# A hybrid encoder layer on one core: memory of its own for the output product's splits, FNet sums over even and odd columns, Conformer taps emitted one per quarter block

## The chip, the cores and the metric

The kernel runs on one core of a Trainium2 chip. Its time is the device time of one execution in microseconds (us); of several executions the median counts. One more execution is recorded by the hardware profiler: the profile and its trace. In it, PE is TensorE's matmuls and PEld its weight loads, DVE is VectorE, ACT is ScalarE, POOL is GpSimd, SP is the queue that issues most transfers, and L112 is line 112 of the kernel.

## What is computed

One layer over 512 positions of width 2048, in float32. A normalised `h` goes through one input projection of 11264 columns into four groups of 1024 channels and a gate; the groups are normalised, gated, and projected back:

```python
proj = h @ w_in
a, f, hy, q, gate = split(proj)                  # 2G, G, 3G, G, 4G columns, G = 1024
u = a_val * sigmoid(a_gate)                      # Conformer
u = depthwise_conv(u, conv_dw_w, conv_dw_b)      # 31 taps
y_a = silu(layer_norm(u)) @ conv_pw_w + conv_pw_b
ff = fft2(f, norm="ortho").real                  # FNet
y_b = ff @ fnet_w + fnet_b
hy = depthwise_conv(hy, hy_short_w, hy_short_b)  # Hyena, 3 taps
v, x1, x2 = split(hy)
for o, g_o in enumerate((x1, x2)):
    z = g_o * long_conv(z, kf[:, o], hy_skip[o]) # z is v at first
y_c = z
y_m = attention(q, mem_n @ mem_wk, mem_n @ mem_wv)
y = rms_norm(concat(y_a, y_b, y_c, y_m), per group) * silu(gate)
out = x + rms_norm(y @ w_out, post_g)
```

## The kernel before, in words

Channels stand on the 128 partitions and positions on the 512 columns, so a group is eight channel tiles (`CT`). To keep float32 accuracy, each operand of a large product is split in two parts: `split` (L79, L80) writes the high part with a ScalarE copy and the low part with a VectorE subtraction, and `mm3` (L112 to L114) makes three matmuls of them, high by high, high by low and low by high. `load` (L87) brings a weight block into one of three staging buffers, and `wload` splits it; `wload_dma` (L106 to L108) does so with a transfer that adds on the way, for the Hyena projections. `project(b)` (L313) makes one projection of 128 output channels: 48 matmuls of 512 columns in four quarters of 12, and after each quarter it advances a generator `fill` if it is given one.

There is no hand-written order: the program is written stage by stage, a scheduler sets each engine's queue from it, and a tile of a memory pool that reuses a buffer waits for the last reader of the old contents. A pool that is opened when another is closed takes over its memory, and waits likewise. The stages around the change:

- Hyena loop (`for ct in range(CT)`): three projections with a short convolution (`short`, L548, L549), then two `long_conv`. A `long_conv` goes: sum and difference `pq` on VectorE (L568, L569), four transposes on TensorE (L573), split `tH`, `tL`, 24 matmuls of 256 columns, products with the filter on VectorE, split `wwH`, `wwL`, matmuls again, four transposes (L624), and the output with its gate (L629, L630). Then `group_square` squares the result on ScalarE (L484) and adds it on POOL (L485) to `gaccC`. In four of the eight tiles (`CONV1`) a Conformer projection (`conv_proj`) and its 31 taps (`conv_taps`, L525, 30 operations of VectorE) follow. After the loop the projections left in `early` are made (`project_early`).
- FNet: 16 blocks of `w_f` are folded and multiplied (L681 to L697); in block 1 `group_norm` takes column sums of `gaccC` (L158) and spreads the scale with four small matmuls on `diag` (L152, L153). Then the transform over the positions: cosine tables `cg` (four chunks of 128 and a chunk of alternating signs) by the folded `eeH`, `eeL`, 30 matmuls of two columns (L743, L744), and sine tables `sg` by `ooH`, `ooL`. `out_product` multiplies with the FNet weights (L798 to L801).
- Conformer layer norm (pool `wp5`): the mean is subtracted (L952) in eight tiles, and `group_square` sums the squares in `vacc`; column sums of it (L158) come after the gate projection that follows. `lnt` holds mean, scale and two squares. The pointwise product sums its squares in `gaccA` likewise. Last, `group_scale` (L500) and a product with the early gates (L998) finish the group in 15 operations.
- Output product (pool `wp4`, opened when `wp5` is closed): in five rounds, 32 channel tiles `y` are split into `jh`, `jl` (three buffers each) and multiplied with `wo`.

Of the kernel before, what the change touches and what calls it, by code (L numbers as in the profile page):

```python
# [12 lines left out]
F32R = mybir.dt.float32r  # L13
# [7 lines left out]
P = 128  # L21
# [4 lines left out]
KD = D // P  # L26
# [12 lines left out]
C3 = 2.0 * math.pi - C1 - float(np.float32(C2))  # L39


@with_exitstack
def encoder_kernel(ctx: ExitStack, tc: tile.TileContext, a: dict, out: bass.AP):
# [26 lines left out]
    def pg():  # L70
        return psg.tile([P, 512], F32, tag="pg", name=nm("pg"))
# [289 lines left out]
    def query_early(i):  # L361
        ps = project(40 + i)
# [4 lines left out]
    def gate_early(i):  # L367
        ps = project(48 + i)
# [191 lines left out]
    def long_conv(z, g, dst, o, ct):  # L560
# [8 lines left out]
        dve.tensor_tensor(pq[:, 1], z0, z1, op=sub)  # L569
        pt = pg()  # L570
# [5 lines left out]
        split(tH, tL, pt)  # L576

# [31 lines left out]
        split(wH, wL, w_)  # L609
        pd = pg()  # L610
# [9 lines left out]
        dve.tensor_tensor(th_[:, 1], pdv[:, 0], dif, op=sub)  # L620
        pc = pg()
# [10 lines left out]
    gacc = cst.tile([P, 512], F32, tag="gacc", name="gaccC", bufs=2)  # L632
    for ct in range(CT):
        v = short(16 + 3 * ct, ct)
        x1 = short(16 + 3 * ct + 1, CT + ct)
        x2 = short(16 + 3 * ct + 2, 2 * CT + ct)
        z = kb[1][:, 2 + ct % 2, :]
        long_conv(v, x1, z, 0, ct)
        y = yC[ct // 4][:, ct % 4, :]
        long_conv(z, x2, y, 1, ct)  # L640
        group_square(y, gacc, wt("pp", bufs=3), ct == 0)
        if ct in CONV1:
            conv_proj(CONV1.index(ct), ub)
            conv_taps(CONV1.index(ct), ub)
    project_early(len(early))
# [81 lines left out]
    NS = ((0, 128), (128, 256), (130, 258))  # L727
    psT = [pg() for _ in range(3)]
    psX = pg()
    for c in range(5):  # L730
        raw = load(a["cg"][c], 512)
        th, tl = wsplit(raw[:, 0:512])
        for n in range(3):
            s = slice(*NS[n])
            if c < 4:
                mm3(psT[n], eeH[:, c, s], eeL[:, c, s], th, tl, c == 0, False)
            else:
                pe.matmul(psT[n], eeH[:, c, s], th, start=False, stop=False)
                pe.matmul(psT[n], eeL[:, c, s], th, start=False, stop=True)
# [51 lines left out]
    def out_product():  # L791
        for hf in range(2):
            psE = [pg() for _ in range(4)]
            psO = [pg() for _ in range(2)]
            for k in range(4):
# [177 lines left out]
    for hf in range(2):  # L973
# [54 lines left out]
    for r, ms in rounds:  # L1028
# [5 lines left out]
        for kp in range(16):  # L1034
# [12 lines left out]
            for kk in range(2):  # L1047
# [11 lines left out]
                jh = wt("jh", dt=F32R, bufs=3)  # L1059
                jl = wt("jl", dt=F32R, bufs=3)  # L1060
# [16 lines left out]
def _tables():  # L1077
# [10 lines left out]
    c = np.arange(512)  # L1088
    ang = 2.0 * np.pi * (np.outer(c, c) % 1024) / 1024.0
    alt = np.tile((-1.0) ** c / P, (P, 1))  # L1090
    t["cg"] = np.concatenate([np.cos(ang).reshape(4, P, 512), alt[None]])
    t["sg"] = np.sin(ang).reshape(4, P, 512)
# [24 lines left out]
def _arrange(inp):  # L1117
# [24 lines left out]
    r["w_f"] = np.concatenate([wf[:, :512], wf[:, mir]], axis=1).reshape(KD, P, 1024)  # L1142
# [7 lines left out]
    r["fw"] = np.stack([fw[:512], fw[mir]]).reshape(2, 4, P, 2, 512).transpose(3, 1, 2, 0, 4).reshape(2, 4, P, 1024)  # L1150
# [46 lines left out]
```

## Time and profile before

| | us |
|---|---|
| three runs | 1713.63, 1719.39, 1721.88 |
| median | 1719.39 |
| the profiled execution, its own time | 1716.29 |
| its span in the trace | 1714.5 |
| TensorE busy, of the span | 1655.3 (97%) |
| VectorE busy | 1221.9 (71%) |
| ScalarE busy | 813.6 (47%) |
| GpSimd busy | 189.9 (11%) |

A busy TensorE need not be at its peak: matmuls are pipelined, so one row's duration is longer than the distance to the next, and what a matmul costs is read from the distance of two starts. The granted clock is given in parts of 2.4 GHz; 0.50 is the lower level, 1.2 GHz. "[11.19 <-ACT jh L79]" behind a row says how long the engine had been idle before it and which instruction ended that.

### The profile page before, as it was taken

Reading aid. Unit: us, or ns where it says so; the run is one execution under the profiler, and the core shown is the slowest. Engines: PE = TensorE matmul, PEld = TensorE weight load, DVE = VectorE, ACT = ScalarE, POOL = GpSimd, SP = SyncE. Lnnn points to the kernel's source line nnn. Section 1 sums busy time; section 2 is a strip of 40 time slices with the busy share of each in tenths; the row PEclk is TensorE's granted clock in tenths of the full one; section 3 lists DMA queues with packets and bytes.
Section 4 is the critical chain, followed back from the end, with each engine's and each line's share of the span. In section 5 each row is a group of like instructions: output and inputs, shape, how many; then the busy total and the mean of one; then the engine's idle time right before and its main releaser. Section 6 shows DMA issues by size and latency. Waiting matters only on the chain.

```text
span 1714.5 us, 21887 instructions
## 1 busy us (share of the span) xinstructions
PE 1655.3 (97%) x8201; PEld 1386.6 (81%) x8201; DVE 1221.9 (71%) x1835; ACT 813.6 (47%) x1185; POOL 189.9 (11%) x146
## 2 busy tenths in 40 slices
PE   7999999999999999999999999999999699999997
PEld 5997888887777778878888888888878588888876
DVE  7866987378797887989874979985562545454586
ACT  6645655344343443424344355445454434444564
POOL 5101422011020120100000020100212000000000
PEclk9999999999999999999999999999999899999999
DMA  8654545768576684623434334232123523222355
GB/s 290 227 185 156 160 139 158 218 155 176 136 171 150 146 181 126 137 93 106 134 105 133 105 124 153 81 111 86 62 98 109 193 98 102 93 101 98 128 203 179
DMA packets 87487, 240.27 MB, mean 140 GB/s; under 512 B 8915, under 2 KB 26579, under 8 KB 86869
## 3 DMA queue, kind: packets, MB, share of 16 engines
q1 hardware_dynamic: 80468, 213.70, 38.6%
q0 software_dynamic: 6912, 25.17, 7.9%
q8 instruction: 64, 1.05, 0.2%
q14 instruction: 43, 0.34, 0.1%
HBM read 220.21 MB, written 18.63 MB: 139 GB/s over the span
## 4 chain that ended last, share of the span: by engine, by line
PE 78%; DVE 14%; DMA 2%; issue 2%; ACT 2%; POOL 1%; SPq 0%; DVEq 0%; ACTq 0%; POOLq 0%
PE pf L114 14%; PE pf L112 14%; PE pf L113 14%; PE pg L113 11%; PE pg L112 11%; PE pg L114 11%; DVE y L525 5%; DVE wl L80 2%; DVE yc L629 1%; DMA raw<-in_wv_dram 1%; POOL vacc L485 1%; ACT wh L79 1%; DMA wl<-in_w_std_dram 1%; DVE y L630 1%; DVE pq L568 1%
## 5 line engine op out<-in xcount | busy, mean ns | idle before, releaser
L112 PE MATMUL pf<-hH,wh 128*128 128x512 f32 x1280 | 505.6, 395 | 0.0
L114 PE MATMUL pf<-hH,wl 128*128 128x512 f32 x1280 | 502.7, 393 | 0.3 <-DMA wl<-in_w_std_dram 0.3
L113 PE MATMUL pf<-hL,wh 128*128 128x512 f32 x1280 | 502.1, 392 | 0.0
L80 DVE TENSOR_TENSOR wl<-raw,wh 128x1024 fp32r<-128x1024 f32 (+1 forms) x240 | 304.0, 1269 | 151.6 <-ACT wh L79 151.0
L79 ACT ACTIVATE wh<-raw 128x1024 fp32r<-128x1024 f32 (+1 forms) x240 | 247.5, 1033 | 231.3 <-PE pf L113 140.8
L114 PEld LDWEIGHTS pf<-hH,wl 128*128 128x128 f32 x1280 | 241.5, 189 | 49.6 <-DMA wl<-in_w_std_dram 0.7
L113 PEld LDWEIGHTS pf<-hL,wh 128*128 128x128 f32 x1280 | 241.9, 189 | 46.9 <-issue 0.2
L112 PEld LDWEIGHTS pf<-hH,wh 128*128 128x128 f32 x1280 | 241.7, 189 | 46.9 <-issue 0.5
L80 DVE TENSOR_TENSOR jl<-y,jh 128x512 fp32r<-128x512 f32 (+1 forms) x154 | 91.3, 597 | 121.6 <-ACT jh L79 120.5
L79 ACT ACTIVATE jh<-y 128x512 fp32r<-128x512 f32 (+1 forms) x154 | 84.4, 550 | 178.6 <-PE pg L113 113.4
L112 PE MATMUL pg<-wh,jh 128*128 128x512 f32 x384 | 150.6, 392 | 11.2 <-ACT jh L79 11.2
L113 PE MATMUL pg<-wl,jh 128*128 128x512 f32 x384 | 150.5, 392 | 0.0
L114 PE MATMUL pg<-wh,jl 128*128 128x512 f32 x384 | 150.4, 392 | 0.0
L107 ACT ACTIVATE wh<-raw 128x1024 fp32r<-128x1024 f32 x48 | 51.0, 1061 | 99.8 <-PE pf L113 51.8
L525 DVE SCALAR_TENSOR_TENSOR y<-ubuf,par,y 128x512 f32<-128x512 f32 x120 | 93.0, 775 | 3.5 <-ACT y L523 1.5
L112 PEld LDWEIGHTS pg<-wh,jh 128*128 128x128 f32 x384 | 72.8, 189 | 26.6 <-ACT jh L79 11.5
L114 PEld LDWEIGHTS pg<-wh,jl 128*128 128x128 f32 x384 | 72.6, 189 | 15.2 <-DVE jl L80 0.2
L113 PEld LDWEIGHTS pg<-wl,jh 128*128 128x128 f32 x384 | 72.7, 189 | 15.1
L108 POOL DMA_DIRECT2D wl<-in_w_std_dram x48 | 41.7, 870 | 286.2 <-ACT wl L106 274.3
L106 ACT ACTIVATE wl<-raw 128x1024 fp32r<-128x1024 f32 x48 | 50.2, 1046 | 0.0
L525 DVE SCALAR_TENSOR_TENSOR y<-ub,par,y 128x512 f32<-128x512 f32 x60 | 46.4, 773 | 2.3 <-ACT y L523 1.1
L1016 POOL TENSOR_TENSOR xres<-xres,og 128x512 f32<-128x512 f32 x4 | 6.7, 1682 | 372.2 <-ACT og L1015 372.2
(380 smaller groups left out, 2916.8 us busy)
## 6 DMA issues: line engine op xcount, KB each, us to landing
raw<-in_w_std_dram SPq DMA_DIRECT2D x160, 512.0 KB, 4.2
raw<-in_wo_dram SPq DMA_DIRECT2D x77, 512.0 KB, 3.3
wl<-in_w_std_dram POOLq DMA_DIRECT2D x48, 512.0 KB, 7.8
raw<-in_wk_dram SPq DMA_DIRECT2D x16, 512.0 KB, 4.0
kd<-y SPq DMA_DIRECT2D x16, 512.0 KB, 4.9
y<-kd SPq DMA_DIRECT2D x32, 256.0 KB, 6.0
raw<-in_w_f_dram SPq DMA_DIRECT2D x16, 512.0 KB, 3.2
raw<-in_wv_dram SPq DMA_DIRECT2D x15, 512.0 KB, 5.2
```

The lines of the kernel that those rows point to most:

```text
L79: act.activation(h, src, AF.Copy)
L80: dve.tensor_tensor(l, src, h, op=sub)
L106: act.activation(l, raw, AF.Copy, scale=-1.0)
L107: act.activation(h, raw, AF.Copy)
L108: pool.dma_start(l, src, accum_op=add)
L112: pe.matmul(ps, wh, xh, start=start, stop=False)
L113: pe.matmul(ps, wh, xl, start=False, stop=False)
L114: pe.matmul(ps, wl, xh, start=False, stop=stop)
L485: pool.tensor_tensor(acc, sqt, acc, op=add)
L525: dve.scalar_tensor_tensor(o, u[:, t:t + L], conv_w[:, ct, t:t + 1], o, op0=mul, op1=add)
L568: dve.tensor_tensor(pq[:, 0], z0, z1, op=add)
L629: dve.scalar_tensor_tensor(yv, pcv[:, h], cinv[:, o, ct:ct + 1], yv, op0=mul, op1=add)
```

## The change

**FNet.** The columns of the input are taken in the order even, odd (`FNC`), and the tables have 256 columns instead of 512. A sum over the even and one over the odd columns stand in the two halves of a bank; `both` adds and subtracts them to give all 512. The tables come in three loads instead of nine, the two-column sums take 18 matmuls instead of 30. In `out_product` the weights are ordered anew, and in block 0 the first row comes by a transfer from `fw0`.

**Hyena loop.** The taps become a generator with one tap per step, advanced by `project` after every quarter, in the projections of the next tile; `conv_proj` stands ahead of the two convolutions. `long_conv` becomes a generator too, but it is run through at once.

**Layer norm.** The squares go to PSUM and are added on VectorE; mean and scale share one tile, `stat`. The same holds in the pointwise stage.

**Output product.** A pool `wj`, opened ahead of `wp5`, holds two of the three buffers of `jh` and `jl`.

```diff
-    def short(b, j):
-        ps = project(b, how=wload_dma)
+    def short(b, j, fill):
+        ps = project(b, fill, wload_dma)
...
-    def conv_taps(ct, ub):
+    def taps(ct, ub, slow=True):
...
         for t in range(1, W31):
             dve.scalar_tensor_tensor(o, u[:, t:t + L], conv_w[:, ct, t:t + 1], o, op0=mul, op1=add)
+            if slow:
+                yield
...
+    def conv_pair(ct, v, x1, x2):
+        z = kb[1][:, 2 + ct % 2, :]
+        yield from long_conv(v, x1, z, 0, ct)
+        y = yC[ct // 4][:, ct % 4, :]
+        yield from long_conv(z, x2, y, 1, ct)
+        group_square(y, gacc, wt("pp", bufs=3), ct == 0)
+    work = {"taps": iter(())}
+    def advance():
+        while True:
+            next(work["taps"], None)
+            yield
+    fill = advance()
     for ct in range(CT):
-        v = short(16 + 3 * ct, ct)
-        x1 = short(16 + 3 * ct + 1, CT + ct)
-        x2 = short(16 + 3 * ct + 2, 2 * CT + ct)
-        z = kb[1][:, 2 + ct % 2, :]
-        long_conv(v, x1, z, 0, ct)
-        y = yC[ct // 4][:, ct % 4, :]
-        long_conv(z, x2, y, 1, ct)
-        group_square(y, gacc, wt("pp", bufs=3), ct == 0)
+        vx = [short(16 + 3 * ct + i, i * CT + ct, fill) for i in range(3)]
         if ct in CONV1:
-            conv_proj(CONV1.index(ct), ub)
-            conv_taps(CONV1.index(ct), ub)
-    project_early(len(early))
+            conv_proj(CONV1.index(ct), ub, fill)
+        for _ in conv_pair(ct, *vx):
+            pass
+        if ct in CONV1:
+            for _ in work["taps"]:
+                pass
+            work["taps"] = taps(CONV1.index(ct), ub)
+    project_early(len(early), fill)
+    for _ in work["taps"]:
+        pass
...
-    for c in range(5):
-        raw = load(a["cg"][c], 512)
-        th, tl = wsplit(raw[:, 0:512])
+    cgH, cgL = wload(a["cg"][:, 0:1024])
+    raw = load(a["cg"][:, 1024:1280], 256)
+    caH, caL = wsplit(raw[:, 0:256], 256)
+    for c in (0, 1, 4, 2, 3):
+        h = c // 2 % 2
+        v = slice(256 * h, 256 * h + 256)
         for n in range(3):
             s = slice(*NS[n])
             if c < 4:
-                mm3(psT[n], eeH[:, c, s], eeL[:, c, s], th, tl, c == 0, False)
+                w_ = slice(256 * c, 256 * c + 256)
+                mm3(psT[n][:, v], eeH[:, c, s], eeL[:, c, s], cgH[:, w_], cgL[:, w_], c % 2 == 0, c == 3)
...
-        for c in range(5):
+        for c in (0, 1, 4):
...
+    def both(ps, odd_first):
+        o_ = wt("odd", (P, 256), bufs=1)
+        act.activation(o_, ps[:, 256:512], AF.Copy)
+        t = wt("bth", bufs=1)
+        dve.tensor_tensor(t[:, 0:256], ps[:, 0:256], o_, op=add)
...
-        split(teH[:, n, 0:512], teL[:, n, 0:512], psT[n])
+        split(teH[:, n, 0:512], teL[:, n, 0:512], both(psT[n], False))
...
                 if k == 0:
-                    act.activation(we[0:1, :], raw[0:1, 0:512], AF.Copy)
+                    sp.dma_start(we[0:1, :], a["fw0"][hf:hf + 1, :])
...
+    wj = ctx.enter_context(tc.tile_pool(name="wj", bufs=2))
     w5 = ctx.enter_context(ExitStack())
     wp = w5.enter_context(tc.tile_pool(name="wp5", bufs=1))
-    lnt = wt("lnt", (P, 4, 512), bufs=1)
...
-    mean = lnt[:, 0, :]
-    rstd = lnt[:, 1, :]
+    mean = rstd = wt("stat", bufs=1)
...
-        group_square(y, vacc, lnt[:, 2 + ct % 2, :], ct == 0)
+        sq = vacc if ct == 0 else pg()
+        act.activation(sq, y, AF.Square)
+        if ct:
+            dve.tensor_tensor(vacc, sq, vacc, op=add)
...
-                jh = wt("jh", dt=F32R, bufs=3)
-                jl = wt("jl", dt=F32R, bufs=3)
+                jp, nb = (wj, 2) if r == 0 or n % 3 else (wp, 1)
+                jh, jl = (jp.tile([P, 512], F32R, tag=t, name=nm(t), bufs=nb) for t in ("jh", "jl"))
```

The order of the instructions, at three places. First VectorE in the Hyena loop, before, around the second `pq` of a tile; L525 are taps, L548 and L549 the short convolution:

```order
L568 TENSOR_TENSOR pq_4661<-vx_4521 128x256
L525 SCALAR_TENSOR_TENSOR y_526_3004<-ubuf,par,y_526_3004 128x512
L569 TENSOR_TENSOR pq_4661<-vx_4521 128x256
L525 SCALAR_TENSOR_TENSOR y_526_3004<-ubuf,par,y_526_3004 128x512 x4
L548 SCALAR_TENSOR_TENSOR vx_4588<-pf_4525,par,vx_4588 128x511
L525 SCALAR_TENSOR_TENSOR y_526_3004<-ubuf,par,y_526_3004 128x512
L549 SCALAR_TENSOR_TENSOR vx_4588<-pf_4525,par,vx_4588 128x511
L525 SCALAR_TENSOR_TENSOR y_526_3004<-ubuf,par,y_526_3004 128x512 x11
L548 SCALAR_TENSOR_TENSOR vx_4655<-pf_4592,par,vx_4655 128x511
L525 SCALAR_TENSOR_TENSOR y_526_3004<-ubuf,par,y_526_3004 128x512
L549 SCALAR_TENSOR_TENSOR vx_4655<-pf_4592,par,vx_4655 128x511
L80 TENSOR_TENSOR tL_4670<-pg_4664,tH_4669 128x512
```

And with the change, around a `pq` in a tile with taps (L529 are taps, L646 the gate, L558 the short convolution):

```order
L529 SCALAR_TENSOR_TENSOR y_526_3004<-ubuf,par,y_526_3004 128x512
L646 TENSOR_TENSOR y_532_3019<-yc_4333,vx_4047 128x512
L529 SCALAR_TENSOR_TENSOR y_526_3004<-ubuf,par,y_526_3004 128x512
L578 TENSOR_TENSOR pq_4340<-y_532_3019 128x256
L579 TENSOR_TENSOR pq_4340<-y_532_3019 128x256
L529 SCALAR_TENSOR_TENSOR y_526_3004<-ubuf,par,y_526_3004 128x512
L578 TENSOR_TENSOR pq_4642<-vx_4494 128x256
L579 TENSOR_TENSOR pq_4642<-vx_4494 128x256
L84 TENSOR_TENSOR tL_4349<-pg_4343,tH_4348 128x512
L529 SCALAR_TENSOR_TENSOR y_526_3004<-ubuf,par,y_526_3004 128x512 x2
L558 SCALAR_TENSOR_TENSOR vx_4565<-pf_4498,par,vx_4565 128x511
L529 SCALAR_TENSOR_TENSOR y_526_3004<-ubuf,par,y_526_3004 128x512
```

The run of taps ahead of `tL` is gone there; single taps stand between the steps of the convolutions, one ahead of the two parts of `pq_4340` and one behind them. The second place is TensorE at the end of the loop, before. `pf` is a projection's bank, `jh` and `jl` are FNet's folded input of a block:

```order
L114 MATMUL pg_6920<-jh_6930,wl_6940 128x256
L112 MATMUL pg_6920<-jh_6930,wh_6939 128x256
L113 MATMUL pg_6920<-jl_6931,wh_6939 128x256
L114 MATMUL pg_6920<-jh_6930,wl_6940 128x256
L158 MATMUL pf_7002<-ones,gaccC 128x1 x4
L112 MATMUL pg_6915<-jh_6976,wh_6985 128x258
L113 MATMUL pg_6915<-jl_6977,wh_6985 128x258
L112 MATMUL pg_6916<-jh_6976,wh_6985 128x258
```

With the change:

```order
L116 MATMUL pf_6827<-hH,wh_6862 128x512
L117 MATMUL pf_6827<-hL,wh_6862 128x512
L118 MATMUL pf_6827<-hH,wl_6863 128x512
L162 MATMUL pf_7002<-ones,gaccC 128x1 x4
L116 MATMUL pg_6915<-jh_6930,wh_6939 128x258
L117 MATMUL pg_6915<-jl_6931,wh_6939 128x258
L116 MATMUL pg_6916<-jh_6930,wh_6939 128x258
L117 MATMUL pg_6916<-jl_6931,wh_6939 128x258
```

The column sums of `gaccC` (L158, now L162) stood behind the 24 matmuls of FNet's first block and stand ahead of them now, right behind the last projection, of which 30 matmuls stood behind the last transposes and 12 do now. The third place is the start of the output product: VectorE before,

```order
L500 SCALAR_TENSOR_TENSOR y_1871_11198<-y_1871_11198,par,rsg_11551 128x512 x2
L998 TENSOR_TENSOR y_1871_11198<-y_1871_11198,uL_11472 128x512 x2
L500 SCALAR_TENSOR_TENSOR y_1872_11199<-y_1872_11199,par,rsg_11551 128x512 x2
L998 TENSOR_TENSOR y_1872_11199<-y_1872_11199,uL_11472 128x512 x2
L500 SCALAR_TENSOR_TENSOR y_1872_11199<-y_1872_11199,par,rsg_11551 128x512
L998 TENSOR_TENSOR y_1872_11199<-y_1872_11199,uL_11472 128x512
L80 TENSOR_TENSOR jl_11613<-y_529_3016,jh_11612 128x512
L80 TENSOR_TENSOR jl_11629<-y_529_3016,jh_11628 128x512
L80 TENSOR_TENSOR jl_11651<-y_529_3016,jh_11650 128x512
```

and with the change:

```order
L504 SCALAR_TENSOR_TENSOR y_1870_11189<-y_1870_11189,par,rsg_11542 128x512 x2
L1060 TENSOR_TENSOR y_1870_11189<-y_1870_11189,uL_11463 128x512 x2
L504 SCALAR_TENSOR_TENSOR y_1871_11190<-y_1871_11190,par,rsg_11542 128x512 x2
L1060 TENSOR_TENSOR y_1871_11190<-y_1871_11190,uL_11463 128x512 x2
L504 SCALAR_TENSOR_TENSOR y_1871_11190<-y_1871_11190,par,rsg_11542 128x512
L84 TENSOR_TENSOR jl_11642<-y_529_3016,jh_11641 128x512
L1060 TENSOR_TENSOR y_1871_11190<-y_1871_11190,uL_11463 128x512
L84 TENSOR_TENSOR jl_11658<-y_529_3016,jh_11657 128x512
L84 TENSOR_TENSOR jl_11680<-y_530_3017,jh_11679 128x512
```

Before, the first two pairs `jl` stood behind the 15 closing operations (the gains L500 and the products with the early gates L998); now it is the third `jl` that stands behind 14 of them, and the first two stand far ahead, before the first subtraction of the layer norm.

## Rows read from the trace of the kernel before

**Rows 1.** The page, section 1: busy us (share of the span) x instructions of each engine.
```profile
PE 1655.3 (97%) x8201; PEld 1386.6 (81%) x8201; DVE 1221.9 (71%) x1835; ACT 813.6 (47%) x1185; POOL 189.9 (11%) x146
```

**Rows 2.** TensorE's waits, whole span: us in total, times, longest us.
```profile
PE pg L112 <- ACT jh L79: 11.2, 1, 11.2
...
PE pg L113 <- DVE tL L80: 4.9, 6, 1.5
PE pg L573 <- DVE pq L568: 4.4, 8, 0.6
PE pg L158 <- POOL vacc L485: 3.5, 1, 3.5
```

**Rows 3.** Stretches of the span: busy by engine, granted clock, DMA share, GB/s.
```profile
core 0: us, PE busy (x) PEld busy (x) DVE busy (x) ACT busy (x) POOL busy (x), PEclk, DMA share, GB/s
899.40:909.30 9.90, 9.90 (x44) 8.07 (x43) 4.76 (x10) 4.30 (x10) 0.00 (x0) 1.00 0.41 112
909.30:912.60 3.30, 3.30 (x31) 3.26 (x30) 0.90 (x2) 0.63 (x1) 0.00 (x0) 1.00 0.60 196
912.60:916.70 4.10, 4.10 (x13) 3.23 (x13) 2.42 (x6) 2.33 (x6) 0.00 (x0) 0.59 0.35 124
337.00:772.00 435.00, 425.36 (x2070) 344.53 (x2068) 355.89 (x554) 183.86 (x226) 50.40 (x51) 1.00 0.62 146
...
1247.10:1251.00 3.90, 0.40 (x3) 0.01 (x1) 1.96 (x2) 3.87 (x5) 3.22 (x3) 1.00 0.00 0
1251.00:1258.00 7.00, 7.00 (x23) 6.00 (x24) 4.27 (x8) 1.96 (x3) 0.00 (x0) 0.52 0.45 148
1340.20:1351.85 11.65, 0.46 (x4) 0.16 (x2) 9.72 (x16) 1.28 (x3) 0.00 (x0) 0.50 0.73 305
1351.85:1357.00 5.15, 5.15 (x12) 4.05 (x13) 3.89 (x9) 2.88 (x9) 0.00 (x0) 0.50 0.37 103
```

**Rows 4.** Timeline of TensorE, FNet's first block: start us, us, engine, line, operation, tiles.
```profile
781.52 0.28 PE L112 MATMUL pg<-jh,wh 128*128 128x256 f32 x1
...
781.87 0.28 PE L113 MATMUL pg<-jl,wh 128*128 128x256 f32 x1
```

**Rows 5.** Timeline at the FNet weights' block 0, VectorE and ScalarE.
```profile
972.66 0.42 DVE L80 TENSOR_TENSOR faL<-pg,faH 128x258 fp32r<-128x258 f32 x1
...
973.44 0.63 ACT L79 ACTIVATE wh<-web 128x512 fp32r<-128x512 f32 x1
```

**Rows 6.** DMA issues: times, KB each, us from issue to landing.
```profile
fwp<-in_fwp_dram SPq DMA_DIRECT2D x1, 128.0 KB, 2.5
```

**Rows 7.** Timeline at the start of the output product, VectorE and TensorE.
```profile
1350.36 0.69 DVE L998 TENSOR_TENSOR y<-y,uL 128x512 f32<-128x512 f32 x1
...
1351.85 0.80 PE L112 MATMUL pg<-wh,jh 128*128 128x512 f32 x1 [11.19 <-ACT jh L79]
```

**Rows 8.** Timeline of the layer norm's sums, VectorE and POOL.
```profile
1232.70 2.73 DVE L500 SCALAR_TENSOR_TENSOR y<-y,par,rsg 128x512 f32<-128x512 f32 x4
1235.35 4.30 DVE L952 TENSOR_TENSOR y<-y,lnt 128x512 f32<-128x512 f32 x7
...
1236.84 12.29 POOL L485 TENSOR_TENSOR vacc<-lnt,vacc 128x512 f32<-128x512 f32 x6 [15.70 <-ACT lnt L484]
```

**Rows 9.** Timeline of the Hyena loop, VectorE's taps and the matmul behind them.
```profile
395.15 9.41 DVE L525 SCALAR_TENSOR_TENSOR y<-ubuf,par,y 128x512 f32<-128x512 f32 x12
...
405.14 0.68 DVE L80 TENSOR_TENSOR tL<-pg,tH 128x512 fp32r<-128x512 f32 x1
...
405.87 0.39 PE L113 MATMUL pg<-tL,mtab 128*128 128x256 f32 x1 [0.41 <-DVE tL L80]
```

**Rows 10.** Timeline from the end of the Hyena loop into FNet, POOL and TensorE.
```profile
775.25 1.29 POOL L485 TENSOR_TENSOR gaccC<-pp,gaccC 128x512 f32<-128x512 f32 x1 [39.58 <-ACT pp L484]
...
780.47 0.36 PE L112 MATMUL pg<-jh,wh 128*128 128x258 f32 x1 [1.21 <-issue]
...
786.04 0.39 PE L112 MATMUL pg<-jh,wh 128*128 128x258 f32 x1 [1.65 <-ACT wh L79]
```

More of the change, by code (lines that the diff above doesn't have):

```diff
@@ L39 @@
 C3 = 2.0 * math.pi - C1 - float(np.float32(C2))
+FNC = np.concatenate([np.arange(0, 512, 2), np.arange(1, 512, 2)])
 @with_exitstack
@@ L359, in encoder_kernel, with query_early @@
     w0.close()
-    def query_early(i):
-        ps = project(40 + i)
+    def query_early(i, fill):
+        ps = project(40 + i, fill)
         t = cst.tile([P, 512], F32, tag="sgt", name=nm("sgt"))
@@ L365, in query_early, with gate_early @@
         sp.dma_start(qdm[:, i, :], t)
-    def gate_early(i):
-        ps = project(48 + i)
+    def gate_early(i, fill):
+        ps = project(48 + i, fill)
         t = cst.tile([P, 512], F32, tag="sgt", name=nm("sgt"))
@@ L529, in conv_taps @@
             pool.tensor_tensor(csum, o, csum, op=add)
+    def conv_taps(ct, ub):
+        for _ in taps(ct, ub, False):
+            pass
     ub = yp.tile([P, 3, 544], F32, tag="y5", name="ubuf")
@@ L576, in long_conv @@
         split(tH, tL, pt)
+        yield
         pse = [pg(), pg()]
@@ L609, in long_conv @@
         split(wH, wL, w_)
+        yield
+        yield
+        yield
         pd = pg()
@@ L620, in long_conv @@
         dve.tensor_tensor(th_[:, 1], pdv[:, 0], dif, op=sub)
+        yield
         pc = pg()
@@ L735, in encoder_kernel @@
             if c < 4:
-                mm3(psT[n], eeH[:, c, s], eeL[:, c, s], th, tl, c == 0, False)
-            else:
-                pe.matmul(psT[n], eeH[:, c, s], th, start=False, stop=False)
-                pe.matmul(psT[n], eeL[:, c, s], th, start=False, stop=True)
+                w_ = slice(256 * c, 256 * c + 256)
+                mm3(psT[n][:, v], eeH[:, c, s], eeL[:, c, s], cgH[:, w_], cgL[:, w_], c % 2 == 0, c == 3)
+            else:
+                pe.matmul(psT[n][:, v], eeH[:, c, s], caH, start=False, stop=False)
+                pe.matmul(psT[n][:, v], eeL[:, c, s], caH, start=False, stop=True)
     for n in range(3):
         s = slice(*NS[n])
-        for c in range(5):
+        for c in (0, 1, 4):
             pe.matmul(psX[:, 2 * n:2 * n + 2], eeH[:, c, s], cgxH[:, 2 * c:2 * c + 2], start=(c == 0), stop=False)
@@ L745, in encoder_kernel @@
     psS = [pg() for _ in range(2)]
+    sgH, sgL = wload(a["sg"])
     for c in range(4):
-        raw = load(a["sg"][c], 512)
-        th, tl = wsplit(raw[:, 0:512])
+        v = slice(256 * (c // 2), 256 * (c // 2) + 256)
+        w_ = slice(256 * c, 256 * c + 256)
         for n in range(2):
             s = slice(P * n, P * n + P)
-            mm3(psS[n], ooH[:, c, s], ooL[:, c, s], th, tl, c == 0, c == 3)
+            mm3(psS[n][:, v], ooH[:, c, s], ooL[:, c, s], sgH[:, w_], sgL[:, w_], c % 2 == 0, c % 2 == 1)
     conv_proj(4, ubm)
+    def both(ps, odd_first):
[3 more added lines that the diff above has]
+        dve.tensor_tensor(t[:, 0:256], ps[:, 0:256], o_, op=add)
+        if odd_first:
+            dve.tensor_tensor(t[:, 256:512], o_, ps[:, 0:256], op=sub)
+        else:
+            dve.tensor_tensor(t[:, 256:512], ps[:, 0:256], o_, op=sub)
+        return t
     teH = wpo.tile([P, 3, 514], F32R, tag="eeH", name="teH")
@@ L760, in encoder_kernel @@
     for n in range(2):
-        split(toH[:, n, :], toL[:, n, :], psS[n])
+        split(toH[:, n, :], toL[:, n, :], both(psS[n], True))
     gate(2, 6, yC)
@@ L985, in encoder_kernel @@
             act.activation(y, accs[m], AF.Identity, bias=pw_b[:, ct:ct + 1])
-            group_square(y, gacc, lnt[:, 2 + ct % 2, :], ct == 0)
+            sq = gacc if ct == 0 else rstd
+            act.activation(sq, y, AF.Square)
+            if ct:
+                dve.tensor_tensor(gacc, sq, gacc, op=add)
     gA = wt("uL", (P, CT, 512), F32, 1)
@@ L1087, in _tables @@
     t["etab"] = e.reshape(4, 2, P, 256).transpose(2, 0, 1, 3).reshape(P, 2048)
[L1088 to L1092, printed above, removed]
+    ang = 2.0 * np.pi * (np.outer(FNC, i) % 1024) / 1024.0
+    alt = np.tile((-1.0) ** i / P, (P, 1))
+    t["cg"] = np.concatenate([np.cos(ang).reshape(4, P, 256).transpose(1, 0, 2).reshape(P, 1024), alt], axis=1)
+    sin = np.sin(ang)
+    sin[256:, 0] = (-1.0) ** i
+    t["sg"] = sin.reshape(4, P, 256).transpose(1, 0, 2).reshape(P, 1024)
     cgx = np.zeros((P, 5, 2))
@@ L1149, in _arrange @@
     fw = v["fnet_w"][0]
-    r["fw"] = np.stack([fw[:512], fw[mir]]).reshape(2, 4, P, 2, 512).transpose(3, 1, 2, 0, 4).reshape(2, 4, P, 1024)
+    j = np.arange(1, 256)
+    k0 = np.concatenate([[256], j, [512], 512 - j])
+    k1 = np.concatenate([[768], 1024 - j, [512], 512 + j])
+    r["fw0"] = fw[0].reshape(2, 512)
+    r["fw"] = np.stack([fw[k0], fw[k1]]).reshape(2, 4, P, 2, 512).transpose(3, 1, 2, 0, 4).reshape(2, 4, P, 1024)
     par["fn_b"] = cm(v["fnet_b"][0])
```

15 lines of the change are left out of this document (10 added, 5 removed).

## The prediction

> **What bounds the kernel now.** I read the busy shares first: TensorE is busy for 1655.3 us of a 1714.5 us span [rows 1], so the time can change in two ways only: fewer or shorter matmuls, or less waiting in front of them. The list of TensorE's waits comes second. Its longest single wait, 11.2 us, is for the split `jh` of the output product; the late `tL` of the Hyena loop adds up to 4.9 us, `pq` to 4.4 us, `vacc` to 3.5 us [rows 2]. Third come the tables by stretch, which show what a wait costs beyond itself: behind the idle 3.90 us at 1247.1 the granted clock is 0.52 (the 1.2 GHz level) for 7.0 us, and behind the 11.65 us at 1340.2 it is 0.50 for 5.15 us [rows 3]. VectorE, 1221.9 us busy [rows 1], is no bound on average, but it ends three of those four waits. Own time of the profiled execution: 1716.29 us; the sum is made against that.
>
> **1. FNet sums over even and odd columns.** 36 cosine, 6 `alt` and 24 sine matmuls, 66 in all, go from 512 to 256 columns. 44 matmuls of 512 columns take 9.90 us, 0.225 each [rows 3]; of 256 columns three steps take 0.35 us, 0.117 each [rows 4]. 66 x 0.108 = 7.1 us less. The two-column matmuls go from 30 to 18; 30 take 3.30 us [rows 3], so 12 fewer are 1.3 us less. Behind them 13 matmuls take 4.10 us at clock 0.59 [rows 3] where 13 x 0.225 is 2.9, a loss of 1.2. Since their run shrinks to 2.0 us, I take 1.0 of that back (0 to 1.2). Term: -9.4 (-8.4 to -9.6). The five new `both` (one ScalarE copy, two VectorE operations of 256 columns each) lie beside four projections of 48 matmuls, 43 us at 0.225; they cost nothing, and without that cover some 1.2 us each, three operations of about 0.42 [rows 5] in a row. Nine table loads become three on SP's queue, which no row shows waited for here.
>
> **2. The first row of the FNet weights comes by a transfer** instead of a ScalarE copy of 0.63 us; the split `wh<-web` follows at 973.44 [rows 5]. A 128 KB load lands in 2.5 us [rows 6]; so the split starts near 975.2, and 1.8 us of delay meets a 1.1 us projection remainder ahead of it plus the 12 `faH` matmuls (12 x 0.12 = 1.4). I take +0.5 (0 to +2.0); late next would be the splits behind it.
>
> **3. Own memory for the output product's splits.** From 1340.2 to 1351.85 TensorE is busy for 0.46 us, while VectorE, busy for 9.72, runs the last gains and products, until 1351.05 [rows 3, 7]: the first `jh` waits for memory that they still read, and its matmul starts at 1351.85 [rows 7]. In the new order the first two splits stand ahead of the Conformer's normalisation, so 24 matmuls plus 8 of the next channel block, 32 x 0.227 = 7.3 us, run inside the gap. Then they need a `jl` queued behind 14 of VectorE's 15 operations, due near 1350.4 + 0.7 = 1351.1, 0.75 before the first matmul of now. 7.3 + 0.75 = 8.0. The idle rest, 1347.5 to 1351.1, is still 3.6 us, like the one at 1247; so of the slow stretch (12 matmuls in 5.15 us against 2.7, a loss of 2.4) I take only 1.0 back. Term: -9.0 (0 to -10.4). The later rounds keep three buffers in total, and round 0's two are refilled during 12 matmuls, 2.7 us, against a split of 1.3: no cost.
>
> **4. Squares of the layer norm added on VectorE.** POOL's six adds take 12.29 us while VectorE's seven subtractions, need 4.30 [rows 8]; `vacc` comes near 1251, and TensorE loses 3.66 us idle plus 3.0 at the low clock (15 long matmuls at 0.43 instead of 0.23) [rows 3]. Now VectorE does, from 1232.7 on, 7 subtractions (4.3), 5 group gains (2.73 / 4 each, 3.4 [rows 8]), 7 adds out of PSUM (between the 0.61 of a subtraction and the 0.68 of a split out of PSUM [rows 8, 9], 4.6) and one gate product (0.7): 13.0, ready at 1245.7. The column sums stand 8 matmuls earlier, at 1247.3 - 1.8 = 1245.5. So 0.2 is left, and I allow 0.9 for the split `wl` that is now queued behind these adds. Term: -5.5 (0 to -6.6). The same adds in the pointwise stage lie beside a gate projection of 10.9 us.
>
> **5. The Hyena loop.** Here TensorE is idle for 435.0 - 425.4 = 9.6 us in all [rows 3]; that is the most the new order can give. Now the 30 taps of a tile stand in bursts: twelve take 9.41 us, 0.78 each, and the matmul on `tL` behind one waits 0.41 us [rows 9], in the worst case 1.5 [rows 2]. One tap per quarter block takes the bursts away: -4.9. The wait for `pq` I leave as it is: there are now 16 to 18 projection matmuls ahead of the transposes instead of 10 (1.4 to 1.8 us more cover), but two taps (1.57) stand in VectorE's chain there. New is a tap ahead of `wwL`, where 5 matmuls cover: half a tap, 0.39, in the 8 convolutions that have taps, +3.1. Term: -1.8 (-9.3 to +7.8).
>
> **6. End of the loop.** After the last transposes 30 projection matmuls (6.8 us) and FNet's first 24 now stand ahead of the column sums; in the new order 12 (2.7 us), then at once the column sums of `gaccC`. The chain of VectorE, ScalarE and POOL is the same: POOL's sum ends at 776.54, FNet's first matmul starts at 780.47, its second block at 786.04 [rows 10]. TensorE gets there with 18 fewer matmuls in hand: 18 x 0.227 = +4.1 (+1.0, if the chain moves forward with the taps gone, to +7.0, if the clock falls too).
>
> Sum: -9.4 + 0.5 - 9.0 - 5.5 - 1.8 + 4.1 = -21.1; 1716.3 - 21.1 = 1695.2. The median of before is 1719.39; its three runs and the profiled one average 1717.8, 1.5 above the own time, so the forecast is **1696.7 us**.
>
> **The clock at the new gap.** The row: 3.7 us idle at 1247 was followed by 7.0 us at clock 0.52 [rows 3]; term 6 leaves idle stretches of about 1.6 and 3.4 us ahead of FNet's 24 matmuls. At 0.24 instead of 0.12 each these would take 2.9 us more, part of which the wait for the second block absorbs; by that the time is 1699.6. The Trainium skill, TensorE: Matmul & The Clock Gate, section on HAM oscillation, says that gaps between bursts of matmuls put the engine back to its lower rate, so that the next burst starts cold; by that rule the changed order pays at the loop's end, and this trace agrees at 1247 and 1340.
>
> **The rivals.** (a) The clock falls at the new gap, as just said: 1699.6. For it: every longer gap of the trace; against: the second block's wait hides most. Chance 0.12.
> (b) The taps move the wait, not end it: in each of 8 convolutions one tap of 0.78 is uncovered at two places, 12.5 us in place of 3.1: 1706.1. For it: `pq` waits in 8 places already [rows 2]; against: the wider spacing. 0.15.
> (c) More comes back: all 9.3 us of the loop's waits (7.5 better than taken) and both low stretches: about 1687. 0.14.
> (d) The splits do not run early, because the memory is not the only thing that holds them: term 3 is nothing, 1705.7. Against: the new order has them ahead. 0.06.
> (e) Slower: VectorE becomes the loop's bound. With taps between every pair of steps, two of them (1.57) uncovered at three waits (`pq`, `tL`, `wwL`) in 8 convolutions, 24 x 1.57 = 37.7 instead of 3.1: 1731.3. It passes no change from (22.7 + 3.1) / 24 = 1.08 us per wait. Against: VectorE is busy 355.9 of 435 us there [rows 3]. 0.03.
>
> **How the numbers follow.** The forecast has 0.50, with 1690 to 1703 as its own range. What a measurement of this kernel can tell from no change is about 0.5%, so faster means under 1710.8 and slower over 1728. Faster: 0.50 + 0.12 + 0.14 + 0.05 of (d) + 0.07 of (b), whose scatter of 4 us and further uncovered taps put the rest above 1710.8: 0.88. Same: 0.08 + 0.01 = 0.09. Slower: 0.03. The range goes from (c) less the 4 us by which the fastest run lies under the average, 1682, to (b) plus as much, 1710; outside lie (e), the upper part of (b) and edges, about 0.16.
>
> **What would show it.** FNet's cosine and sine stretch shorter by 8 us; one column-sum wait on `vacc` under 1 us; at the output product's start 32 matmuls before a wait of 3 to 4 us on `jl`; no `tL` wait over 0.5 us in the loop; a new wait of about 5 us on `gaccC` and `jh` at the loop's end. I am wrong if TensorE's idle in the loop grows beyond 13 us, or if the gap at the output product stays over 8 us.

## The result and the profile after

The changed kernel takes 1694.13 us (median of four runs, 1692.63 to 1696.15) against 1718.13 us before (1713.63 to 1721.88): ratio 0.9862, 95% interval 0.9835 to 0.9889. The forecast was 1696.7, in a range from 1682 to 1710.

In the busy shares of the page, the changed kernel's TensorE has 12 matmuls less and 10 us less of busy time; VectorE's load is the same and POOL's smaller [rows 1]:

```profile
PE 1645.1 (97%) x8189; PEld 1378.5 (81%) x8189; DVE 1221.2 (72%) x1855; ACT 813.0 (48%) x1184; POOL 166.6 (10%) x132
```

Where the time went is read by places that both programs have, as the starts of matmuls in the two profiled executions (us from the span's start):

| start of | before | after | difference | gained in between |
|---|---|---|---|---|
| the column sums ahead of the Hyena loop (L461, now L465) | 304.06 | 305.60 | +1.54 | +1.5 |
| FNet's first block | 780.47 | 784.32 | +3.85 | +2.3 |
| the first cosine matmul | 899.40 | 904.36 | +4.96 | +1.1 |
| the product after the sine stretch | 963.37 | 958.30 | -5.07 | -10.0 |
| the Conformer mean's sum | 1230.34 | 1226.93 | -3.41 | +1.7 |
| the first pointwise matmul | 1280.73 | 1270.26 | -10.47 | -7.1 |
| the output product's fourth channel tile | 1362.56 | 1341.79 | -20.8 | -10.3 |
| the last matmul | 1704.15 | 1683.24 | -20.9 | -0.1 |

The first line is not the change: up to there the two programs have the same instructions, and in the thirteen recorded executions of this study that place lies between 302.36 and 306.20. So the loop and its end cost 2.3 us here, and a difference of 1 or 2 us between two traces can be the executions' own.

The list of TensorE's waits after, the lines that answer to [rows 2] (us in total, times, longest us):

```profile
PE pg L116 <- ACT wh L83: 11.7, 4, 6.1
...
PE pg L584 <- DVE pq L578: 3.1, 8, 1.1
...
PE pg L118 <- DVE jl L84: 2.2, 1, 2.2
PE pg L116 <- ACT wwH L83: 2.1, 3, 0.7
...
PE pf L118 <- DMA wl<-in_w_std_dram: 1.5, 1, 1.5
PE pg L117 <- DVE tL L84: 1.5, 7, 0.2
PE pf L162 <- POOL gaccC L489: 1.4, 1, 1.4
```

The wait of 11.2 us for `jh` and that of 3.5 us for `vacc` are gone, `tL` fell from 4.9 to 1.5 us; `wwH` rose from 0.2 to 2.1, and `gaccC` is new. The first row was 8.2 us in three waits before; the 2.77 us ahead of FNet's first block, shown below, are now in it. The table by stretch after, to be read beside [rows 3]:

```profile
core 0: us, PE busy (x) PEld busy (x) DVE busy (x) ACT busy (x) POOL busy (x), PEclk, DMA share, GB/s
784.30:789.90 5.60, 5.58 (x25) 5.49 (x26) 5.60 (x15) 1.90 (x3) 0.00 (x0) 0.50 0.32 99
...
1328.80:1332.50 3.70, 3.70 (x14) 2.98 (x13) 1.92 (x5) 0.60 (x1) 0.00 (x0) 0.55 1.01 421
...
1242.00:1256.00 14.00, 14.00 (x72) 11.80 (x71) 13.37 (x23) 9.39 (x14) 0.00 (x0) 1.00 0.46 152
```

The low clock at the layer norm is gone: from the column sums on (1242 to 1256) it is 1.00, and TensorE is never idle. At FNet's first block it is new; before, the second block had one of 3.42 us (the row below). At the start of the output product it is shorter, and it now lies ahead of a wait, no longer behind one.

```profile
786.98:790.40 3.42, 3.42 (x19) 3.42 (x18) 3.03 (x9) 1.06 (x2) 0.00 (x0) 0.50 0.21 73
```

Behind the two-column sums, where before 13 matmuls had 0.59 [rows 3], the clock now stays up:

```profile
907.40:909.40 2.00, 1.97 (x17) 1.97 (x18) 0.54 (x2) 0.95 (x2) 0.00 (x0) 1.00 0.76 213
909.40:911.90 2.50, 2.50 (x25) 2.50 (x23) 1.93 (x4) 1.80 (x3) 0.00 (x0) 1.00 0.35 141
911.90:914.80 2.90, 2.90 (x27) 2.90 (x27) 2.68 (x6) 1.14 (x4) 0.00 (x0) 1.00 0.66 230
```

The end of the loop, in the timeline of POOL and of TensorE (start, us, engine, line), which answers to [rows 10]: the last transposes, the wait of the column sums, the first block's start, and the second block, now without a wait of its own. Behind them stand the last transposes before.

```profile
779.18 1.26 POOL L489 TENSOR_TENSOR gaccC<-pp,gaccC 128x512 f32<-128x512 f32 x1 [22.30 <-ACT pp L488]
```
```profile
775.63 0.70 PE L640 MATMUL pg<-ident,t 128*128 128x128 f32 x4
...
780.49 1.05 PE L162 MATMUL pf<-ones,gaccC 128*128 128x1 f32 x8 [1.42 <-POOL gaccC L489]
784.32 0.58 PE L116 MATMUL pg<-jh,wh 128*128 128x258 f32 x1 [2.77 <-ACT wh L83]
...
789.98 0.37 PE L116 MATMUL pg<-jh,wh 128*128 128x258 f32 x1
```
```profile
771.72 0.69 PE L624 MATMUL pg<-ident,t 128*128 128x128 f32 x4
```

From the last transposes to FNet's first block it is 8.75 us before and 8.69 after. TensorE's matmuls behind the transposes, 30 before and 12 now, do not set this time; the chain of the other engines that makes its operands does.

And the start of the output product, TensorE, which answers to [rows 7]. After the first of the rows 31 more matmuls run; then TensorE waits for the third `jl`:

```profile
1328.81 0.47 PE L116 MATMUL pg<-wh,jh 128*128 128x512 f32 x1
...
1340.75 1.20 PE L118 MATMUL pg<-wh,jl 128*128 128x512 f32 x4 [2.20 <-DVE jl L84]
```

### The profile page after: what moved, and what is told of

It is laid out like the page before. It is cut to its first block, busy times and chain, and to the rows that moved or that the text cites. A ratio compares the mean times of both kernels' runs of the same rounds, so it can differ in the third digit from the quotient of the medians.

```text
span 1694.4 us, 21825 instructions
## 1 busy us (share of the span) xinstructions
PE 1645.1 (97%) x8189; PEld 1378.5 (81%) x8189; DVE 1221.2 (72%) x1855; ACT 813.0 (48%) x1184; POOL 166.6 (10%) x132
## 3 DMA queue, kind: packets, MB, share of 16 engines
q8 instruction: 64, 1.05, 0.2%
## 4 chain that ended last, share of the span: by engine, by line
PE 79%; DVE 11%; DMA 4%; issue 3%; ACT 2%; SPq 0%; POOL 0%; DVEq 0%; ACTq 0%; POOLq 0%
PE pf L118 15%; PE pf L117 15%; PE pf L116 15%; PE pg L117 11%; PE pg L116 11%; PE pg L118 11%; DVE y L529 3%; DVE wl L84 2%; DMA wl<-in_w_std_dram 1%; DMA raw<-in_wv_dram 1%; ACT wh L83 1%; DVE yc L645 1%; PE pg L584 1%; DMA kdm<-mst 0%; DMA y<-in_xT_dram 0%
## 5 line engine op out<-in xcount | busy, mean ns | idle before, releaser
L84 DVE TENSOR_TENSOR wl<-raw,wh 128x1024 fp32r<-128x1024 f32 (+2 forms) x234 | 293.4, 1257 | 116.2 <-ACT wh L83 115.6
L83 ACT ACTIVATE wh<-raw 128x1024 fp32r<-128x1024 f32 (+2 forms) x234 | 244.4, 1046 | 204.4 <-PE pf L117 129.5
L529 DVE SCALAR_TENSOR_TENSOR y<-ubuf,par,y 128x512 f32<-128x512 f32 x120 | 92.4, 770 | 1.0
L440 POOL TENSOR_TENSOR y<-fsq,y 128x512 f32<-128x512 f32 x24 | 44.5, 1856 | 42.0 <-ACT fsq L439 41.9
```

The source lines that it names most:

```text
L83: act.activation(h, src, AF.Copy)
L84: dve.tensor_tensor(l, src, h, op=sub)
L440: pool.tensor_tensor(acc, sq, acc, op=add)
```

## The experiments

My theory after the result: the parts act each at its own place, FNet, the layer norm and the splits give about 27 us there, and the Hyena part gives back some 4. The runs bear out the places, but neither of the two sums. The rival: the order of the taps carries part of the gain, or the later gains hang on each other.

**FNet's part alone**, in the kernel before:

```diff
-        split(teH[:, n, 0:512], teL[:, n, 0:512], psT[n])
+        split(teH[:, n, 0:512], teL[:, n, 0:512], both(psT[n], False))
...
-                    act.activation(we[0:1, :], raw[0:1, 0:512], AF.Copy)
+                    sp.dma_start(we[0:1, :], a["fw0"][hf:hf + 1, :])
```


> The kernel before with the FNet part of the change alone (even and odd columns, both, the weights' first row by a transfer). If the parts act each at its own place, the trace of the whole change gives this part 10.0 us (from the first cosine matmul, 4.96 us behind, to the end of the sine stretch, 5.07 us ahead): 10 us less than before, and no other stretch moves by more than 1 us. If part of that stretch's gain was borrowed from the other parts (the loop's end hands over later blocks), 6 to 8 us less.

Measured: ratio 0.9944 (0.9929 to 0.9959), 9.6 us less. From the first cosine matmul (898.37) to the product after the sine stretch (951.98) it is 10.4 us shorter than before; the rest of the trace is within 1 us up to the layer norm. This part stands by itself.

**The layer norm's part alone** (with the pointwise stage's adds, whose squares go to the tile `stat`, not to PSUM):

```diff
-        group_square(y, vacc, lnt[:, 2 + ct % 2, :], ct == 0)
+        sq = vacc if ct == 0 else pg()
+        act.activation(sq, y, AF.Square)
+        if ct:
+            dve.tensor_tensor(vacc, sq, vacc, op=add)
```


> The kernel before with the layer norm's and the pointwise stage's squares added on VectorE, mean and scale in one tile, and nothing else. If the parts act each at its own place: 7 us less, all of it between the sum of the means and the first pointwise matmul. If VectorE's adds were only early because the output product's first splits had been moved as well, under 4 us less.

Measured: 0.9971 (0.9961 to 0.9981), 5.0 us less (3.3 to 6.7); in the traces the first pointwise matmul moves from 0.87 us late to 6.19 early, 7.1 us. The 7 us that I expected lie just outside the interval of the runs, which does not exclude the other expectation, under 4; the stretch in the trace is what speaks for the 7, and why the runs show less is open. The last add, in the timeline of VectorE, is done 0.4 us before the column sums' first matmul at 1246.39; nothing waits for it:

```profile
1245.29 0.68 DVE L955 TENSOR_TENSOR vacc<-pg,vacc 128x512 f32<-128x512 f32 x1
```

**The same with the pool for the splits** (the pool needs memory that the layer norm's part sets free, so it was not tried alone):

```diff
+    wj = ctx.enter_context(tc.tile_pool(name="wj", bufs=2))
...
+                jp, nb = (wj, 2) if r == 0 or n % 3 else (wp, 1)
```


> As the run with the layer norm's part alone, plus the pool of its own for two of three buffers of the output product's splits (it needs the memory that the layer norm's part sets free). If the splits are what the start of the output product waited for: 10.3 us less than the layer norm's part alone, 17.4 us less than before, with 32 matmuls ahead of a wait of about 2 us on jl. If VectorE's 15 closing operations bound the start whatever the memory, under 3 us less than the layer norm's part alone.

Measured: 0.9907 (0.9890 to 0.9924), 11.0 us less than the layer norm's part alone; in the traces 10.4 us between the first pointwise matmul and the fourth channel tile. TensorE's timeline there has the forecast wait:

```profile
1330.62 0.71 PE L153 MATMUL pg<-diag,ones 128*128 128x128 f32 x4 [2.72 <-DVE diag L152]
1342.96 1.20 PE L114 MATMUL pg<-wh,jl 128*128 128x512 f32 x4 [2.11 <-DVE jl L80]
```

So it was memory that the first splits waited for, not VectorE's 15 closing operations.

**The Hyena part alone**:

```diff
...
+        vx = [short(16 + 3 * ct + i, i * CT + ct, fill) for i in range(3)]
         if ct in CONV1:
-            conv_proj(CONV1.index(ct), ub)
-            conv_taps(CONV1.index(ct), ub)
-    project_early(len(early))
+            conv_proj(CONV1.index(ct), ub, fill)
+        for _ in conv_pair(ct, *vx):
+            pass
+        if ct in CONV1:
+            for _ in work["taps"]:
+                pass
+            work["taps"] = taps(CONV1.index(ct), ub)
```


> The kernel before with the Hyena part alone (taps one per quarter, conv_proj ahead of the convolutions). My theory after the result: inside the loop it gives and takes the same (within 2 us), and the loop's end costs 3 to 4 us, so 3 to 5 us slower than before. Rival: one tap at a time is worth the 4.9 us of the tL waits and the loop's end only 3, so 2 us faster.

Measured: 1.0005 (0.9992 to 1.0017): no difference that can be told, from 1.4 us faster to 2.9 slower. Both expectations lie outside or at the edge of that; no gain from the part can be told, and it is less of a loss than I had read from the one trace, where 1.54 of the 3.85 us stood ahead of the loop. From that place to FNet's first block this run's trace has 0.5 us more than before. Its waits are those of the whole change (`tL` 1.4, `pq` 3.0, `wwH` 2.2, `gaccC` 1.4 us).

**The whole change without the Hyena part**, against **the whole change again** on the same chip:

> The whole change without its Hyena part (taps in bursts, conv_proj behind the convolutions, 30 projection matmuls behind the loop's last transposes). If the parts add up, FNet -9.6, layer norm -5.0 and the splits -11.0 give 25.6 us less than before, 1 to 3 us less than the whole change, and the stretch from the loop's end to FNet's last matmul is 3 us shorter than in the whole change. If the tap order carries part of the gain of the whole change, 2 us or more slower than the whole change.

> The whole change again, for comparison on the same chip: 0.985 to 0.988 of before.

Measured: 0.9862 (0.9845 to 0.9879) and 0.9864 (0.9844 to 0.9884). By medians 1692.73 against 1694.75, by spans 1690.8 against 1693.2, but the intervals cover each other, and allow some 4 us either way: the Hyena part is not needed for the gain, and what it costs is not settled. Without it the gain is 23.7 us (20.8 to 26.6), against 25.6 as the sum of the parts' runs; the 27 us of the traces' stretches are outside. The stretch from the loop's end to FNet's end, which I expected 3 us shorter, is not: from the last transposes to the first cosine matmul it is 128.45 us without the part and 128.95 with it. What the Hyena part costs at the loop's end does not lie in that stretch; the 18 matmuls are done ahead of the transposes instead.

**conv_proj back behind the convolutions, taps still one per quarter**; and **conv_proj ahead, taps in bursts**:

```diff
-        if ct in CONV1:
-            conv_proj(CONV1.index(ct), ub, fill)
         for _ in conv_pair(ct, *vx):
             pass
         if ct in CONV1:
+            conv_proj(CONV1.index(ct), ub, fill)
```


> The whole change with conv_proj back behind the two convolutions; the taps stay one per quarter block. 34 projection matmuls then stand behind the loop's last transposes instead of 12. If the loop's end costs what it does because too few matmuls are left there: no wait for gaccC, 3 to 4 us less than the whole change, and tL waits still under 2 us in all. Rival: those 22 matmuls filled waits inside the loop, which come back, and the total is within 1 us of the whole change.

```diff
-            for _ in work["taps"]:
-                pass
-            work["taps"] = taps(CONV1.index(ct), ub)
+            conv_taps(CONV1.index(ct), ub)
```


> The whole change with conv_proj ahead of the convolutions as it is, but the 30 taps of a tile in bursts again. 36 projection matmuls stand behind the last transposes. If the single taps are what took the tL waits away: the tL waits are back at about 4.9 us and wwH under 0.5, with no gaccC wait; in all within 2 us of the whole change. If conv_proj's place did it: tL stays under 2 us.

The first: 0.9844 (0.9827 to 0.9861), 1690.66 us, 4 us under the median of the whole change on the same chip (the intervals overlap). No wait for `gaccC`, as expected; but `tL` waits 4.6 us, where I had expected under 2. VectorE's timeline shows why: written one per quarter, the taps still run twelve in a row, as in [rows 9].

```profile
395.35 9.41 DVE L529 SCALAR_TENSOR_TENSOR y<-ubuf,par,y 128x512 f32<-128x512 f32 x12
404.68 0.75 DVE L558 SCALAR_TENSOR_TENSOR vx<-pf,par,vx 128x511 f32<-128x511 f32 x1
405.34 0.68 DVE L84 TENSOR_TENSOR tL<-pg,tH 128x512 fp32r<-128x512 f32 x1
```

The second: 0.9962 (0.9950 to 0.9975), 16 us slower than the whole change, where I had expected 2 at most. Two of its waits of TensorE, and VectorE's timeline ahead of the longest one for `vx`:

```profile
PE pf L116 <- DVE vx L559: 9.5, 4, 2.5
...
PE pg L117 <- DVE tL L84: 2.3, 6, 0.7
```
```profile
728.13 0.73 DVE L529 SCALAR_TENSOR_TENSOR y<-ubuf,par,y 128x512 f32<-128x512 f32 x1
728.79 0.73 DVE L559 SCALAR_TENSOR_TENSOR vx<-pf,par,vx 128x511 f32<-128x511 f32 x1
```

The next projection's first matmul waits at 729.67 for the second step of the short convolution, which stands behind taps and holds the projection's bank (there are two). So neither half of the Hyena part does what the whole does: with conv_proj behind, single taps leave this run of twelve in VectorE's row; with conv_proj ahead, they are what keeps the banks free. Of the `tL` waits (4.9 us) conv_proj's place alone took away more than half (2.3 left, neither of the two values expected), single taps alone almost nothing (4.6 left), and both together 3.4 (1.5 left).

**The last tile's square in PSUM**, added to `gaccC` on VectorE, with conv_proj behind, and with conv_proj ahead; beside **conv_proj behind again**:

```diff
-        group_square(y, gacc, wt("pp", bufs=3), ct == 0)
+        if ct < CT - 1:
+            group_square(y, gacc, wt("pp", bufs=3), ct == 0)
+        else:
+            sq = pg()
+            act.activation(sq, y, AF.Square)
+            dve.tensor_tensor(gacc, sq, gacc, op=add)
```


> conv_proj behind the convolutions as in the run before, and the last tile's square of the Hyena group goes to PSUM and is added to gaccC on VectorE instead of POOL, so that FNet's first fold no longer waits for POOL to leave the loop's memory. If that wait sets FNet's start: FNet's first block starts 1 to 1.5 us earlier after the last transposes (8.8 us before), the wait for the second block is gone or under 0.5 us, and the kernel is 1 to 4 us faster than with conv_proj behind alone. If the weights' fold and split set it: within 1 us.

> The whole change with the last tile's square in PSUM and its add on VectorE, conv_proj ahead as in the change (12 matmuls behind the last transposes). If the chain over POOL is what is long at the loop's end: the gaccC wait of 1.4 us falls under 0.7 us and FNet's first matmul comes 1 us sooner after the transposes than 8.2 us; 1 to 2 us faster than the whole change.

> conv_proj behind the convolutions again, to compare on the same chip: 0.983 to 0.986 of before.

With conv_proj behind: 0.9839 (0.9822 to 0.9857), 1688.68 us, against 0.9849 (0.9834 to 0.9864), 1690.35 us. FNet's first fold now follows the last gate at once, as VectorE's timeline shows; without it VectorE stood idle for 2.13 us there, until POOL's add was done:

```profile
771.71 0.69 DVE L646 TENSOR_TENSOR y<-yc,vx 128x512 f32<-128x512 f32 x1
772.43 0.69 DVE L717 TENSOR_TENSOR fh<-hH,hL 128x512 f32<-128x512 f32 x1
773.06 0.69 DVE L659 TENSOR_TENSOR gaccC<-pg,gaccC 128x512 f32<-128x512 f32 x1
```

Yet FNet's first matmul comes only 0.5 us sooner after the transposes (8.28 us against 8.76), since now the 34 projection matmuls bind, and the second block 0.9 us sooner. The wait ahead of the second block, which was to be gone or under 0.5 us, is 1.30 us as without it. The gain of 1.7 us by medians lies within both intervals, so it is not shown. This kernel has the lowest ratio of the study, not clear of the other two runs with conv_proj behind.

With conv_proj ahead: 0.9873 (0.9849 to 0.9896), against 0.9862 and 0.9864 for the change in its two measurements; the 1 to 2 us that I expected are not seen. The `gaccC` wait falls to 0.7 us and FNet starts 7.5 instead of 8.7 us after the transposes, as expected; what that gave was lost elsewhere in the recorded execution (last section).

## Why the prediction was right, point by point

- **FNet's sums** (taken: -9.4). Right, 0.4 past its range in the trace: -10.0 in the whole change, 9.6 us by the runs of this part alone. The low clock behind the two-column sums is gone entirely, where I had taken 1.0 of 1.2. `both` cost nothing. The first row by a transfer cost 0.0, where I had taken +0.5: the matmuls behind it are 5.07 us ahead on either side of it.
- **The splits' memory** (-9.0). Right in mechanism and order of size: 10.3 us. 32 matmuls ahead of the wait, as worked out; the wait was 2.2 us instead of 3.6, because TensorE ran part of the 32 at the low clock after the `diag` wait. The term took only 1.0 of the 2.4 us of the old low stretch back, and all 2.4 came back: the new low stretch, some 1.4 us for seven matmuls, only shortens the wait behind it, and behind that wait the clock did not fall (four matmuls in 1.04 us from 1340.75). 7.3 for the 32 matmuls, 2.4, and 0.6 for a third `jl` earlier than the first `jh` was make the 10.3.
- **The layer norm's sums** (-5.5). Mis-sized a little: 7.1 us in both traces, past its range of 6.6, and 5.0 (3.3 to 6.7) by the runs of this part alone. All of the loss came back, 3.5 us of waiting and 3.6 at the low clock, where the term had 3.66 and 3.0; the 0.2 us left and the allowance of 0.9 for the split behind the adds were not needed. The adds out of PSUM take 0.68 us with starts 0.60 apart, the lower bound of the forecast.
- **The Hyena loop** (-1.8) **and its end** (+4.1). The mechanisms came as worked out: `tL` from 4.9 to 1.5 us, `wwH` from 0.2 to 2.1, 12 matmuls and then a new wait for `gaccC` and for FNet's operands. `pq`, which I left as it is, fell by 1.3. The sum of both, +2.3, is what the table has from the place ahead of the loop to FNet's first block, and is inside what the part alone measured (-1.4 to +2.9). It comes apart as the terms do: up to the last transposes 2.4 us more with 18 matmuls (4.1) more done by then, so the loop gained 1.7; and 8.69 us behind them with 18 matmuls fewer, where 4.1 less would have been even, so the end cost 4.0. The two other traces with the Hyena part and POOL's last add (this part alone, the change again) give sums of +0.5 and +1.8, so hitting 2.3 is in part luck. TensorE's idle in the loop fell from 9.6 us to 8.1, where more than 13 would have spoken against the term.
- **The rival on the clock** came true in its mechanism, not in its price: 25 matmuls at 0.50 from 784.3 to 789.9. The rule of the Trainium skill (TensorE: Matmul & The Clock Gate, on HAM oscillation), that a burst behind a gap starts cold, agrees with the trace at this place. It cost nearly nothing, since the second block's operands came no sooner: that block is 3.94 us late, the first 3.85. The low rate used up a wait that was there before (1.65 us, [rows 10]), and the second block no longer runs at it (3.42 us before).
- **Not forecast**: 1.7 us lost between FNet's output and the mean's sum. In the second recorded execution of the changed kernel it is 0.5; the stretch takes 266.87 to 268.63 us in the thirteen recorded executions, and 268.46 and 268.15 are among them from kernels with another Hyena order, so this need not be the change. Also not forecast: 1.1 us between FNet's first block and the first cosine matmul.
- **The total.** The sum was -21.1 and the traces give -20.9; the forecast is 2.6 us from the median. The terms that gave more than taken (splits 1.3, layer norm 1.6, FNet 0.6 and the row of 0.5) are 4.0 us in the trace, and the 4.3 us not forecast, 1.5 of them ahead of the loop, made up for them; so part of the closeness is luck.

## What to carry to other kernels

A pool that opens where another closes passes on the wait of the old tiles' last reader: two pairs of buffers of their own were worth more than any reordering here. How evenly a program emits small operations says little of where they run; the row of the engine's queue says it, and what each one holds (a bank, a buffer) decides what a late one costs. When a change spends filler work earlier, ask what the next stage's start is then covered by: here the chain behind the last transposes took its 8.7 us whether 12 or 30 matmuls stood beside it.

## What the runs showed of the hardware

While POOL added `vacc`, some of VectorE's operations took twice their time. In the kernel before, a gain of 128x512 and a split of 128x1024:

```profile
1236.84 3.97 POOL L485 TENSOR_TENSOR vacc<-lnt,vacc 128x512 f32<-128x512 f32 x1 [15.70 <-ACT lnt L484]
```
```profile
1239.57 1.79 DVE L500 SCALAR_TENSOR_TENSOR y<-y,par,rsg 128x512 f32<-128x512 f32 x1
1241.28 2.31 DVE L80 TENSOR_TENSOR wl<-raw,wh 128x1024 fp32r<-128x1024 f32 x1
```

In the changed kernel, with POOL idle there, the same two took this:

```profile
1239.09 0.74 DVE L504 SCALAR_TENSOR_TENSOR y<-y,par,rsg 128x512 f32<-128x512 f32 x1
...
1241.55 1.21 DVE L84 TENSOR_TENSOR wl<-raw,wh 128x1024 fp32r<-128x1024 f32 x1
```

It went the other way too: POOL's first add, beside VectorE's subtractions that kept their 0.61 us [rows 8], took 3.97 us, where its last took 1.27. So the move to VectorE paid twice, which the forecast had in its durations but did not name. The Trainium skill (SBUF — State Buffer, on the two separate sides) says that GpSimd and a VectorE operation with two SBUF inputs take one pair of ports in turn, each for its whole length; both operations here have two inputs in SBUF, and the 1.05 and 1.10 us that they lost, and the 2.7 us of POOL's add, agree with that.

The recorded execution of the run with conv_proj ahead and the square in PSUM took 1701.96 us, 8.8 above its median. Its table by stretch, and the row of TensorE ahead of it, show a wait of 1.81 us for `cgxH` among short matmuls, and then the lower clock for 13 us although TensorE was busy all the time:

```profile
905.85 0.27 PE L785 MATMUL pg<-cgxH,eeH 128*128 128x2 f32 x1 [1.81 <-ACT cgxH L762]
```
```profile
905.00:907.00 2.00, 1.15 (x6) 1.15 (x7) 0.42 (x1) 0.48 (x2) 0.00 (x0) 0.76 0.70 250
907.00:909.00 2.00, 2.00 (x10) 2.00 (x11) 0.04 (x1) 1.06 (x1) 0.00 (x0) 0.50 0.10 39
909.00:914.00 5.00, 5.00 (x26) 5.00 (x25) 3.16 (x4) 1.44 (x2) 0.00 (x0) 0.50 0.34 105
914.00:919.00 5.00, 5.00 (x24) 5.00 (x25) 1.58 (x5) 1.14 (x4) 0.00 (x0) 0.50 0.31 107
```

In the changed kernel's own trace the same wait is 0.2 us and the clock stays at 1.00, as the rows from 907.40 on in the section on the result show. The trace says why the copy came late: it waited 2.68 us for the transfer of `cgx` (5 KB), which landed 3.9 us after its issue there, against 2.3 us in the changed kernel's own trace. The cosine sums ahead of the two-column ones took 9.90 us before [rows 3] and take some 3 now, too short to cover such a landing: a cost that the forecast did not have. Why the transfer took longer is open.
